# A prefix log-sum-exp whose stores move from SyncE's DMA ring to ScalarE's

## The chip, the cores and the metric

The kernel runs on one core of a Trainium2 chip. The core has a matrix engine (TensorE, PE in the profile), a vector engine (VectorE, DVE), an engine for activation functions (ScalarE, ACT), GpSimd (POOL) and SyncE (SP), which here only starts transfers. Transfers between the large memory (HBM) and the on-chip memory are carried by 16 DMA engines. The metric is the time on the device in microseconds (us), as the median of several executions; lower is better.

## The reference

```python
# x: (4, 4096, 4128) float32
out[:, 0, :] = x[:, 0, :]
for t in range(1, S):
    mx = np.maximum(out[:, t - 1, :], x[:, t, :])
    out[:, t, :] = mx + np.log(np.exp(out[:, t - 1, :] - mx) + np.exp(x[:, t, :] - mx))
```

For each of 4 batches and each of 4128 columns, the output at position t is the logarithm of the sum of the exponentials of all inputs up to t. Input and output are 270.5 MB each.

## The kernel before

A batch has 4096 rows. They are cut into **steps** of 384 rows (128 partitions with R = 3 consecutive rows each) and one of 256 rows per batch (2 rows per partition): 11 steps per batch, 44 in all. In the first batch the short step comes first, in the others last, so steps 0, 21, 32 and 43 are short. A step is one tile `xt` of 128 partitions x 3 x 4128 float32 in the pool `xpool`, which has 4 buffers. The load fills the tile, the exponentials are written over it as 16-bit numbers (the view `half`), the logarithms are written over it again as float32, and the store reads it: one buffer serves a step from the start of its load to the end of its store.

The columns of a step are cut into 4 **chunks** of 1024, the last with a tail of 32 columns more. For a chunk,

- `exp` (L128) is one ScalarE instruction over the chunk's columns of all rows of the step;
- `head` (L132 to L142) sums over the partitions on TensorE into a PSUM tile `pt`, with triangular matrices of ones, and adds the carry of the step before through the matrix `pick`;
- `stage(j)` (L159 to L170) takes the logarithm of row j on ScalarE (L162), then adds the next row's exponentials to `pt` with an identity matrix. The last stage lets VectorE save the running sum in `carry` as two 16-bit parts (`keep`, L92 and L93). In the last chunk, stage 0 also takes the logarithms of the tail (L167).

The order is written out by hand (`manual_schedule`, L85): each engine executes its instructions in the order in which the program emits them. The loop at L192 goes over the chunks of all steps in one sequence. In turn g it emits stage 2 of chunk g-2, stage 1 of chunk g-1 and stage 0 of chunk g, then the exp of chunk g+2, then the head of chunk g+1. So when the last stage of a step's last chunk is emitted, ScalarE's queue already holds before it the exps of the first three chunks of the next step.

Behind the last stage of a step's last chunk stand the step's store and the load of a later step. Before the change both are issued by SyncE, through one DMA ring. Three loads are issued at the start; then load k+3 follows store k on SyncE (L198 to L200). SyncE also works in order: store k waits there until ScalarE has written the last logarithms of step k, and load k+3 stands behind it. Load k+3 uses the buffer of step k-1, so it also waits until store k-1 has landed.

The lines that matter: `load` L109 to L113, `store` L115 and L116, `exp` L126 to L130, `stage` L159 to L170, the first loads L185 to L187, the loop L192 to L205. Transfers are named here by step: load k fills, store k empties the tile of step k.

Of the kernel before, what the change touches and what calls it, by code (L numbers as in the profile page):

```python
# [49 lines left out]
def kernel(  # L50
# [11 lines left out]
    nc = tc.nc  # L62
# [11 lines left out]
    bufs = 4  # L74
# [23 lines left out]
    class Step:  # L98
# [14 lines left out]
            nc.sync.dma_start(out=self.xt, in_=self.dram(x))  # L113

        def store(self):  # L115
            nc.sync.dma_start(out=self.dram(out), in_=self.xt)  # L116

    class Chunk:
        def __init__(self, step, c):
# [52 lines left out]
    steps = []  # L172
# [9 lines left out]
        assert row == S  # L182

    chunks = [Chunk(s, c) for s in steps for c in range(n_main)]
    ahead = bufs - 1  # L185
    for s in steps[:ahead]:
        s.load()  # L187
    stored = 0
    chunks[0].exp()
# [2 lines left out]
    for g in range(len(chunks) + R - 1):  # L192
        for d in range(R - 1, -1, -1):
            if 0 <= g - d < len(chunks) and d < chunks[g - d].t.r:
                k = chunks[g - d]
                k.stage(d)
                if k.c == last and d + 1 == k.t.r:
                    k.t.store()  # L198
                    if stored + ahead < len(steps):
                        steps[stored + ahead].load()  # L200
                    stored += 1
        if g + 2 < len(chunks):
            chunks[g + 2].exp()
        if g + 1 < len(chunks):
            chunks[g + 1].head()  # L205
# [30 lines left out]
```

The softmax here doesn't subtract the row's maximum and nothing guards it: scores larger than these inputs give would overflow.

## Time and profile before

| what | value |
|---|---|
| median of 4 runs | 1263.11 us (1262.47 to 1263.28) |
| profiled execution: its time, its span | 1263.0 us, 1261.3 us |
| busy: ScalarE, TensorE, VectorE | 947.1 us (75%), 688.2 us (55%), 451.5 us (36%) |
| moved | 270.53 MB read, 270.53 MB written, 429 GB/s over the span |
| load of a full step, issue to landing | 42.2 us (median of 40), 6192 KB |
| store of a full step, issue to landing | 28.1 us (median of 40), 6192 KB |
| exp of a chunk of a full step (L128) | 2.77 us; waits for loads 247.7 us in all |
| logarithm of one row of a chunk (L162) | 1.03 us, 512 of them |

The span runs from the first to the last instruction that the profile shows; the execution's own time is 1.7 us longer. An engine's idle time is put down to what ended it. "SPq" is SyncE's queue: its instructions only start transfers, and its waits are shown apart. A line of the timeline has the start, the duration, engine, source line, operation and tiles; in square brackets stands the idle time before it and what ended it. A line of the chain of waits gives shares of the span along the one chain of work that ended last. A line of stretches has the window, its length, the busy time of PE, PE's weight load, DVE, ACT and POOL with their numbers of instructions, the granted TensorE clock, the busy share of the DMA engines and the rate in GB/s.

### The profile page before, as it was taken

The numbers are of one execution on the slowest core, as the hardware profiler recorded it, in microseconds if no ns is written. First come the engines' busy times: TensorE is split into PE (matmuls) and PEld (weight loads), VectorE is DVE, ScalarE is ACT, GpSimd is POOL, SyncE is SP. The second block draws the span as 40 slices with busy tenths as digits, with TensorE's granted clock in tenths as the row PEclk, the third lists the DMA queues.
The fourth block names the chain that finished last, engine by engine and source line by source line (L and its number), as shares of the span: only waits on it lengthen the run. The fifth ranks groups of instructions, "written<-read, shape, count | busy, mean of one in ns | idle before, by whom it ended". The sixth has DMA issues, their size and how long they took to land.

```text
span 1261.3 us, 6165 instructions
## 1 busy us (share of the span) xinstructions
PE 688.2 (55%) x2268; PEld 236.1 (19%) x2268; DVE 451.5 (36%) x445; ACT 947.1 (75%) x733; POOL 2.2 (0%) x13
## 2 busy tenths in 40 slices
PE   3665554565455555555356555555634655555562
PEld 1222111121112111111112121111211211121120
DVE  2443333333333333334424333333442433333344
ACT  5997777777777777778569777777966977777784
POOL 0000000000000000000000000000000000000000
PEclk9887777777787787787768777778767877777776
DMA  9999999999999999999999999999999999999998
GB/s 411 409 431 440 431 428 432 437 431 430 436 434 433 430 437 433 429 431 433 436 431 440 430 429 435 434 431 435 431 432 435 430 430 435 437 430 431 433 423 347
DMA packets 12702, 541.46 MB, mean 429 GB/s; under 512 B 1408, under 2 KB 1408, under 8 KB 1408
## 3 DMA queue, kind: packets, MB, share of 16 engines
q1 hardware_dynamic: 12672, 541.07, 99.4%
q8 instruction: 18, 0.29, 0.1%
q14 instruction: 12, 0.10, 0.0%
HBM read 270.53 MB, written 270.53 MB: 429 GB/s over the span
## 4 chain that ended last, share of the span: by engine, by line
DMA 70%; ACT 21%; PE 5%; issue 2%; DVE 1%; SPq 0%; ACTq 0%
DMA xt<-in_x_dram 67%; ACT xt L128 11%; ACT xt L162 10%; PE pt L88 5%; DMA out_dram<-xt 2%; DVE carry L92 0%; DVE carry L93 0%; ACT xt L167 0%; SPq L116 0%; ACTq L231 0%; SPq L113 0%; ACTq L128 0%; PE qt L88 0%
## 5 line engine op out<-in xcount | busy, mean ns | idle before, releaser
L128 ACT ACTIVATE xt<-xt 128x3072 f16<-128x3072 f32 (+3 forms) x176 | 478.5, 2719 | 247.7 <-DMA xt<-in_x_dram 247.7
L88 PE MATMUL pt<-xt,ident 128*128 128x512 f16 x672 | 249.9, 468 | 531.0 <-ACT xt L162 530.4
L162 ACT ACTIVATE xt<-pt 128x1024 f32<-128x1024 f32 x512 | 487.5, 1030 | 3.0 <-PE pt L88 1.2
L92 DVE CAST carry<-pt 32x1024 f16<-32x1024 f32 x176 | 216.5, 1230 | 761.3 <-ACT xt L162 761.1
L88 PE MATMUL pt<-xt,excl 128*128 128x512 f16 x672 | 247.3, 504 | 0.0
L93 DVE TENSOR_TENSOR carry<-pt,carry 32x1024 f16<-32x1024 f32 x176 | 215.9, 1227 | 6.1
L88 PEld LDWEIGHTS <-ident 128*128 128x128 f16 x672 | 69.9, 104 | 677.3 <-issue 652.9
L88 PE MATMUL pt<-xt,incl 128*128 128x512 f16 x352 | 152.0, 526 | 23.9 <-ACT xt L128 15.1
L88 PEld LDWEIGHTS <-excl 128*128 128x128 f16 x756 | 92.1, 124 | 140.6 <-issue 107.2
L88 PE MATMUL pt<-carry,pick 128*128 128x512 f16 x320 | 110.2, 430 | 0.0
L88 PEld LDWEIGHTS <-incl 128*128 128x128 f16 x480 | 44.7, 111 | 131.2 <-DVE carry L93 95.4
L88 PEld LDWEIGHTS <-pick 128*128 128x128 f16 x360 | 40.7, 113 | 57.5 <-issue 35.3
L167 ACT ACTIVATE xt<-qt 128x96 f32<-128x96 f32 (+1 forms) x44 | 10.9, 248 | 45.8 <-PE pt L88 45.8
L92 DVE CAST carry_t<-qt 32x32 f16<-32x32 f32 x44 | 8.7, 197 | 25.4 <-ACT xt L167 25.2
L88 PE MATMUL qt<-xt,incl 128*128 128x64 f16 (+2 forms) x128 | 12.4, 196 | 0.0
L88 PE MATMUL qt<-xt,excl 128*128 128x64 f16 (+1 forms) x84 | 10.6, 187 | 0.0
L93 DVE TENSOR_TENSOR carry_t<-qt,carry_t 32x32 f16<-32x32 f32 x44 | 8.5, 193 | 1.5
L88 PE MATMUL qt<-carry_t,pick 128*128 128x96 f16 (+1 forms) x40 | 8.2, 205 | 0.0
L83 DVE MEMSET carry<- 128x512 uint32 x4 | 1.9, 485 | 1.1 <-PEq L220 1.0
L70 ACT ACT_TABLE_LOAD x1 | 1.3, 1283 | 0.8 <-PEq L220 0.8
L35 POOL TENSOR_SCALAR_AFFINE_SELECT pick<-pick 128x128 f16<-128x128 f16 x2 | 0.6, 292 | 0.1
L25 POOL TENSOR_SCALAR_AFFINE_SELECT incl<-incl 128x128 f16<-128x128 f16 x1 | 0.3, 292 | 0.0
(11 smaller groups left out, 1.9 us busy)
## 6 DMA issues: line engine op xcount, KB each, us to landing
xt<-in_x_dram SPq DMA_DIRECT2D x40, 6192.0 KB, 42.2
out_dram<-xt SPq DMA_DIRECT2D x40, 6192.0 KB, 28.1
xt<-in_x_dram SPq DMA_DIRECT2D x4, 4128.0 KB, 37.1
out_dram<-xt SPq DMA_DIRECT2D x4, 4128.0 KB, 23.0
```

The source lines that it names most:

```text
L25: nc.gpsimd.affine_select(out=t, in_=t, pattern=[[1, P]], compare_op=mybir.AluOpType.is_ge, fill=0.0, base=base, channel_multiplier=-1,)
L35: nc.gpsimd.affine_select(out=t, in_=t, pattern=[[step, P]], compare_op=mybir.AluOpType.not_equal, fill=1.0, base=base, channel_multiplier=1,)
L70: nc.scalar.preload_act_table_set("natural_log_exp_and_others")
L83: nc.vector.memset(t, 0.0)
L88: nc.tensor.matmul(pt, lhsT=w, rhs=rhs, start=start, stop=stop, skip_group_check=True)
L92: nc.vector.tensor_copy(cr[HI:HI + 32, :], pt[HI:HI + 32])
L93: nc.vector.tensor_tensor(out=cr[LO:LO + 32, :], in0=pt[HI:HI + 32], in1=cr[HI:HI + 32, :], op=mybir.AluOpType.subtract,)
L128: nc.scalar.activation(self.t.half[:, :, 2 * c0:2 * c0 + w], self.t.xt[:, :, c0:c0 + w], ACT.Exp,)
L162: nc.scalar.activation(t.xt[:, j, c * CH:(c + 1) * CH], pt, ACT.Ln)
L167: nc.scalar.activation(t.xt[:, :, t0:D], self.qt, ACT.Ln)
```

## The change

Stores are issued by ScalarE, in its own instruction queue and through its own hardware DMA ring; loads stay with SyncE. All four buffers are loaded at the start, and the load that follows store k is load k+4, into the very buffer that store k empties. SyncE's queue then holds nothing but loads, and each waits only for the store of its slot to land. A store stands on ScalarE behind the last logarithm of its step and ahead of the rest of that turn's work.

```diff
         def store(self):
-            nc.sync.dma_start(out=self.dram(out), in_=self.xt)
+            nc.scalar.dma_start(out=self.dram(out), in_=self.xt)
 ...
     chunks = [Chunk(s, c) for s in steps for c in range(n_main)]
-    ahead = bufs - 1
-    for s in steps[:ahead]:
+    for s in steps[:bufs]:
         s.load()
 ...
                     k.t.store()
-                    if stored + ahead < len(steps):
-                        steps[stored + ahead].load()
+                    if stored + bufs < len(steps):
+                        steps[stored + bufs].load()
                     stored += 1
```

## The prediction

> **What bounds the kernel now.** I read the page first, for the DMA engines' share and rate, then the chain of waits, then SyncE's own waits, then the timelines of SyncE and ScalarE around one step, and last the stretches at the end.
>
> ```profile
> span 1261.3 us, 6165 instructions
> DMA  9999999999999999999999999999999999999998
> q1 hardware_dynamic: 12672, 541.07, 99.4%
> DMA 70%; ACT 21%; PE 5%; issue 2%; DVE 1%; SPq 0%; ACTq 0%
> ```
>
> All 16 DMA engines are busy in every slice, and the one ring that carries loads and stores fills 99.4% of them. The packet records of the same trace (no view prints them one by one) say how full that is: of 10,240 packets of 49,536 bytes the median takes 1.829 us and the next starts 1.826 us after, so 16 engines move 16 x 49,536 / 1.826 = 434 GB/s at best. Each engine carries 8 packets of each transfer: 80 transfers of 3 rows per partition at 8 x 1.826 = 14.61 us and 8 of 2 rows at 8 x 1.219 = 9.75 us make 1168.6 + 78.0 = 1246.6 us. The first packet starts at 1.8 us, the last ends at 1260.0. So the slowest engine has 1260.0 - 1.8 - 1246.6 = 11.6 us beyond its packets, and none of the idle time shown below: instruction fetches (30 packets on queues 8 and 14, each holding its engine up by 0.6 to 1.5 us) and slow packets. The other 15 lose less there and instead stand idle for 0.1 to 7.0 us (4.3 us in the mean) at about 1230, as the stretches show (last columns: PE clock, DMA share, GB/s):
>
> ```profile
> 1225.00:1230.00 5.00, 2.46 (x10) 0.79 (x9) 2.38 (x5) 4.32 (x5) 0.00 (x0) 1.00 0.80 347
> 1230.00:1235.00 5.00, 4.06 (x10) 1.27 (x10) 2.92 (x3) 5.00 (x6) 0.00 (x0) 0.66 0.50 211
> 1235.00:1240.00 5.00, 2.51 (x11) 0.90 (x11) 4.87 (x5) 4.47 (x4) 0.00 (x0) 1.00 0.76 327
> ```
>
> Then the waits on SyncE, and one step on SyncE and ScalarE:
>
> ```profile
> SPq L116 <- ACT xt L162: 1179.2, 44, 30.0
> SPq L113 <- DMA out_dram<-xt: 14.4, 4, 4.9
> ```
> ```profile
> 204.18 0.34 SPq L116 DMA_DIRECT2D out_dram<-xt  x1
> 204.62 0.39 SPq L113 DMA_DIRECT2D xt<-in_x_dram  x1
> 233.64 0.34 SPq L116 DMA_DIRECT2D out_dram<-xt  x1
> ```
> ```profile
> 217.81 2.76 ACT L128 ACTIVATE xt<-xt 128x3072 f16<-128x3072 f32 x1 [6.21 <-DMA xt<-in_x_dram]
> 247.50 2.76 ACT L128 ACTIVATE xt<-xt 128x3072 f16<-128x3072 f32 x1 [6.44 <-DMA xt<-in_x_dram]
> ```
>
> SyncE stands at a store for nearly the whole span, and the next load stands behind it. That looks like the loss, but it isn't one: a store goes out every 29.3 us and lands 28.1 us after its issue (the issue table's median), so the slot of the next load comes free 29.3 - 28.1 = 1.2 us before the store that it stands behind. ScalarE waits 6.4 us per step for a load, because 2 x 14.61 = 29.2 us of transfer per step is more than its own 23 us.
>
> One thing in the order matters later: store k comes late. Load 8 lands at 217.81 and store 7 is issued at 233.64, 15.8 us after it, because ScalarE's order has three exps of step k+1 ahead of the last Ln of step k.
>
> **What the Trainium skill says.** "DMA: Bandwidth & Descriptors", section "Where 436 GB/s comes from": 435 GB/s is the ceiling of the 16 engines; the trace's 434 agrees. Section "Issuing engines are not separate DMA queues": transfers from ScalarE and SyncE run on the same 16 engines and interleave, and a second issuer saves only issue time, here 44 x 0.34 us on SyncE, which is idle. Section "Queues, rings and completion order": an engine goes round the rings that have work, packet by packet. In this trace only instruction fetches show it. "Perfetto Trace Analysis", section "DMA Optimizations", advises separate issuers for input and output for flexibility; this trace shows little for that to free.
>
> **The change part by part.**
>
> *Four loads at the start instead of three.* The engines are busy from 1.8 us either way, and store 0 can't go before 37.2 us, when load 2 is still running. Load 3 moves ahead of store 0; bytes are only reordered. Nothing. Without the cover of full engines it would be worth the 0.4 us of one issue.
>
> *Loads no longer stand behind stores on SyncE.* Worth at most those 1.2 us of lead per load, hidden by the transfers already queued.
>
> *Load k+4 waits for store k to land.* Worked out with the two rings sharing each engine equally: when store k lands, load k+4 is issued and store k+1 is the other stream. Each needs 14.6 us of engine, so both take about 29 us. The load ring runs dry for some 2 us per step (landing 0.6, issue 0.3, first packet 0.85, the last as at the end of this trace: store 42 issued 1233.88, first packet 1234.72), in which the store has the engines alone. The engines run dry only if store k+1 isn't there when store k ends. It is issued 15.8 us after load k+2 lands, and that load ends some 27 us before store k does: 11 us in hand. So the period stays 29.2 us. Nothing.
>
> *44 store issues on ScalarE.* 0.34 us each and about 0.15 us (estimate) for its own last Ln to be written: 44 x 0.5 = 22 us of ScalarE. Behind each stand the Ln and exp of the next chunks, and TensorE and VectorE behind these. The 6.4 us of waiting per step take it. Nothing; with no such idle time it would be 22 us. No store can block ScalarE for its slot's sake, since it waits only for ScalarE's own results; SyncE issued three loads in a row in 1.32 us without being held.
>
> *The end.* Time 0 is store 39's last packet. Load 43 (2 rows, 9.8 us) starts at 1.8; store 40 has 12.8 left by then. Sharing, load 43 ends at 21.4 and lands at 22.0; store 40 ends at 24.4, store 41 (14.6) at 39.0. Store 42 is issued 12.9 us after load 43 lands (1220.94 to 1233.88 before): 22.0 + 12.9 + 0.85 = 35.8, so 3.2 us early. Then 53.7 and, with store 43, 63.4: no gap. If load 42 still has 5 us ahead of load 43, load 43 lands at 30.0, store 41 ends at 43.9 and store 42 starts at 43.8: just in time. The gap at 1230 closes for the 15 engines that have it, but the slowest never had it, and the end is its end. Nothing.
>
> *Reads and writes mixed.* Now an engine alternates load and store packets. Inside the old ring the turn from load to store costs only the 6 ns of the end marker. In about half of the old packets (49%) some engines were already loading while others stored, since the engines drift 4 to 7 us apart: after 60 us these packets exceed the median by 6.0 ns, the others by 2.1. All packets mixed instead of half: 704 packets per engine x 3.9 x 0.51 = +1.4 us. Bounds: 0 if the difference is only that of the fetches among them, and for the alternation itself the rival below.
>
> Sum: profiled execution 1263.0 (span 1261.3 and 1.7 around it; the runs' median is 1263.1), + 0 + 0 + 0 + 0 + 0 + 1.4, on the median: 1264.5.
>
> **The rivals.**
>
> *Alternating rings costs time (slower).* Place: every packet boundary on every engine. The trace has a foreign ring cutting in 29 times: after each instruction fetch the next data packet takes 2.08 to 2.49 us instead of 1.83. Were that 0.25 us the price of every return, 704 x 0.25 = 176 us and 1439 us would result. Against: going into a fetch costs nothing (8192 bytes in 309 ns, the full rate), so I put the delay down to the fetch's own target. It decides from 2.5 / 704 = 3.6 ns per packet. I let the range hold a tenth of the 250, 25 ns: 17.6 us, 1280.7.
>
> *Stores win the sharing (slower).* If stores went first, load 43 would wait for store 40 and for store 41 from its issue at 16, land at about 38, and store 42 would start at 52 instead of 39: +13 us, 1276. For it: the margin of the last step is 0 to 3 us. Against: the equal turns that the skill describes.
>
> *The slowest engine gets rid of its excess (faster).* If fetches and slow packets fell evenly on the engines, the end would come 4.3 us sooner, at 1258.8; all 11.6 us are the limit, 1251.5. For it: other interleaving may shift who is delayed. Against: the instructions and so the fetches stay the same. Full-duplex use of an engine would give far more, but no overlap shows at any of the 40-odd turns from load to store.
>
> **How the numbers follow.** Likeliest case, engines full at the old packet price: 0.55, 1261 to 1267 around 1264.5. Costly alternation 0.23, stores ahead 0.10, less excess 0.12. Faster or slower by 0.2% (2.5 us) is about what a measurement tells from no change; 0.10 of the likeliest case's 0.55 lies beyond 1265.6. So faster 0.12, same 0.45, slower 0.43. The range runs from 1258.5 (the evened-out excess) to 1281 (25 ns per packet); 5 in 100 below, 10 above.
>
> **What would show it.** Right: two rings of about half the engines' time each, DMA at 9 in all slices, ScalarE still waiting 5 to 6 us per step at L128 for loads, loads landing about 29 us after issue, stores up to 40. Packets above 1.83 us net of sharing mean costly alternation; a gap around the last three stores means stores ahead; an 8 in the middle slices means that the coupling of load k+4 to store k starves the rings. Wrong altogether if ScalarE shows long waits at its store issues.

## The result

The changed kernel takes 1265.36 us in the median of 33 runs against 1262.93 us for 54 runs of the kernel before, measured side by side. The ratio of the mean times, without the one run at 1286.29 us that counts as slow, is 1.003, 95% interval 1.0021 to 1.0039; the medians differ by 0.2%. So the change is a small loss, and the forecast of 1264.5 us is 0.9 us off. The runs do something that the forecast does not speak of. Before, all 54 lie between 1262.47 and 1263.41 us. After, the lowest is 1263.60 us, ten of 33 lie above 1268 us, and the highest is at 1286.29 us. So there are two things to explain: a floor 0.8 us higher (profiled execution 1263.83 us against 1263.0), and a spread above that floor, which did not exist before and makes most of the difference in the median.

### The profile page after: what moved, and what is told of

The parts are those of the page before. It is cut to its first block, busy times and chain, and to the rows that moved or that the text cites. A ratio compares the mean times of both kernels' runs of the same rounds, so it can differ in the third digit from the quotient of the medians.

```text
span 1262.1 us, 6084 instructions
## 1 busy us (share of the span) xinstructions
PE 684.9 (54%) x2268; PEld 241.3 (19%) x2268; DVE 451.5 (36%) x445; ACT 951.9 (75%) x733; POOL 2.2 (0%) x13
## 4 chain that ended last, share of the span: by engine, by line
DMA 75%; ACT 20%; PE 3%; issue 0%; DVE 0%; ACTq 0%; SPq 0%
DMA xt<-in_x_dram 40%; DMA out_dram<-xt 35%; ACT xt L128 11%; ACT xt L162 9%; PE pt L88 3%; ACT xt L167 0%; ACTq L116 0%; DVE carry L92 0%; DVE carry L93 0%; SPq L113 0%; ACTq L128 0%; PE qt L88 0%
## 5 line engine op out<-in xcount | busy, mean ns | idle before, releaser
L128 ACT ACTIVATE xt<-xt 128x3072 f16<-128x3072 f32 (+3 forms) x176 | 476.6, 2708 | 226.4 <-DMA xt<-in_x_dram 226.4
L88 PE MATMUL pt<-xt,ident 128*128 128x512 f16 x672 | 254.0, 476 | 540.7 <-ACT xt L162 540.3
L162 ACT ACTIVATE xt<-pt 128x1024 f32<-128x1024 f32 x512 | 492.4, 1024 | 22.0 <-ACT xt L162 12.9
L92 DVE CAST carry<-pt 32x1024 f16<-32x1024 f32 x176 | 216.5, 1230 | 763.3 <-ACT xt L162 763.2
L88 PEld LDWEIGHTS <-incl 128*128 128x128 f16 x480 | 49.3, 113 | 118.6 <-DVE carry L93 72.1
```

Of the source, the lines that this page charges most:

```text
L88: nc.tensor.matmul(pt, lhsT=w, rhs=rhs, start=start, stop=stop, skip_group_check=True)
L92: nc.vector.tensor_copy(cr[HI:HI + 32, :], pt[HI:HI + 32])
L128: nc.scalar.activation(self.t.half[:, :, 2 * c0:2 * c0 + w], self.t.xt[:, :, c0:c0 + w], ACT.Exp,)
L162: nc.scalar.activation(t.xt[:, j, c * CH:(c + 1) * CH], pt, ACT.Ln)
```

## The profile after

The page of the changed kernel: the span, the DMA share and rate in 40 slices, the two rings, the chain, and the two waits on ScalarE that the change touches.

```profile
span 1262.1 us, 6084 instructions
DMA  9999999999999999999999999999999999999997
q1 hardware_dynamic: 6336, 270.54, 49.8%
q10 hardware_dynamic: 6336, 270.54, 49.6%
DMA 75%; ACT 20%; PE 3%; issue 0%; DVE 0%; ACTq 0%; SPq 0%
L128 ACT ACTIVATE xt<-xt 128x3072 f16<-128x3072 f32 (+3 forms) x176 | 476.6, 2708 | 226.4 <-DMA xt<-in_x_dram 226.4
L162 ACT ACTIVATE xt<-pt 128x1024 f32<-128x1024 f32 x512 | 492.4, 1024 | 22.0 <-ACT xt L162 12.9
```

Queue 1 now carries the loads and queue 10, ScalarE's ring, the stores. Each fills half of the engines' time, together 99.4% as the one ring did. The DMA engines stand at 9 in all slices but the last. ScalarE's idle time before L162 grew from 3.0 to 22.0 us: that is the 44 store issues with the wait for the last logarithm before each. Its waiting for loads fell by about the same amount, from 247.7 to 226.4 us. Here is one store of it:

```profile
1213.45 1.04 ACT L162 ACTIVATE xt<-pt 128x1024 f32<-128x1024 f32 x1
1214.52 0.34 ACTq L116 DMA_DIRECT2D out_dram<-xt  x1
1214.91 1.94 ACT L162 ACTIVATE xt<-pt 128x1024 f32<-128x1024 f32 x2 [0.42 <-ACT xt L162]
```

The packet records answer the question of what it costs an engine to alternate. A packet is what one engine moves in one piece, here the rows of one partition: 49,536 bytes in a full step. Around 300 us load and store packets pass through each engine mixed; on 15 of the 16 engines every one of them takes 1.829 us, on the other one up to 1.861. What a packet takes beyond its median is called its excess below. Over the whole run the excess is 5.0 us per engine against 4.7 before.

SyncE waits at the loads now. From issue to landing a store takes longer than before (36.0 us, it was 28.1) and a load less (35.0 us, it was 42.2):

```profile
SPq L113 <- DMA out_dram<-xt: 1165.8, 40, 53.8
```
```profile
xt<-in_x_dram SPq DMA_DIRECT2D x40, 6192.0 KB, 35.0
out_dram<-xt ACTq DMA_DIRECT2D x40, 6192.0 KB, 36.0
```

Last, the stretches around 1230 us, where the engines were idle before:

```profile
1225.00:1230.00 5.00, 2.96 (x17) 1.09 (x16) 2.85 (x4) 4.32 (x6) 0.00 (x0) 1.00 0.92 396
1230.00:1235.00 5.00, 2.65 (x10) 0.89 (x10) 2.46 (x2) 5.00 (x5) 0.00 (x0) 1.00 0.07 23
1235.00:1240.00 5.00, 2.14 (x6) 0.80 (x6) 4.42 (x4) 4.55 (x5) 0.00 (x0) 0.82 0.74 317
```

The gap did not close. It moved and deepened: from 1230 to 1235 nearly nothing moves (23 GB/s). Before, the 16 engines were idle here for 0 to 7.0 us, 4.1 in the mean; now it is 1.2 to 6.4 us, 5.3 in the mean. No engine is spared any more, and that is the higher floor. Before, the engine with the most excess had 10.2 us of it and no idle time; now the one with the most has 10.6 us and 1.2 us of idle time. Store 42 is issued at 1235.48 instead of 1233.88, and the last packet ends at 1260.9 instead of 1260.0.

The timeline of ScalarE says why store 42 is late. These are three first exps of a step (L128) and the stores 41 and 42 between them:

```profile
1198.68 2.76 ACT L128 ACTIVATE xt<-xt 128x3072 f16<-128x3072 f32 x1 [5.41 <-DMA xt<-in_x_dram]
...
1214.52 0.34 ACTq L116 DMA_DIRECT2D out_dram<-xt  x1
...
1222.62 1.91 ACT L128 ACTIVATE xt<-xt 128x2048 f16<-128x2048 f32 x1 [0.15 <-DMA xt<-in_x_dram]
...
1235.48 0.34 ACTq L116 DMA_DIRECT2D out_dram<-xt  x1
```

and the same two exps before the change:

```profile
1196.42 2.76 ACT L128 ACTIVATE xt<-xt 128x3072 f16<-128x3072 f32 x1 [6.16 <-DMA xt<-in_x_dram]
...
1221.02 1.91 ACT L128 ACTIVATE xt<-xt 128x2048 f16<-128x2048 f32 x1 [1.35 <-DMA xt<-in_x_dram]
```

After the change ScalarE waits only 0.15 us for load 43. From the landing of load 42 on it works nearly without a pause: 15.8 us to store 41 and 21.0 us more to store 42. So the end hangs on load **42**, which lands 2.3 us later than before (1198.68 against 1196.42). Of this, 1.2 us come back, since ScalarE no longer waits 1.35 us for load 43, and the wait at store 41 adds 0.4 us: 2.3 - 1.2 + 0.4 = 1.5, of the 1.6 us seen. What delays load 42 was not followed further.

## The experiments

Every run had a kernel before beside it on the same chip, with a median of 1262.87 to 1262.94 us.

**The changed kernel four more times.** No edit. The theories are the end (T), starvation in the middle (M) and, from the third on, disturbance between loads and stores (H).

> The changed kernel as it is, to see its spread. Theory T (the end): every run has its 16 engines full until about 1230 and the loss lies between the landing of load 43 and the issue of store 42; runs differ by when load 43 lands, so the median is 1264 to 1266, a run in four lies above 1269, and in any profile the end is load 43's landing plus 38.4 to 39 us. Rival M (starvation in the middle): long runs show idle DMA engines in the middle slices, at a load that waits for the store of its slot, and the end is as in the short runs.

> The changed kernel once more, for a second trace of it. As for the rerun before: by theory T the end is load 43's landing plus 38.4 to 39 us whatever the time, by rival M idle engines in the middle slices.

> The changed kernel once more, for a trace of a long run: if it lies above 1266 us, rival M wants idle engines in the middle slices, theory H packets longer than 1.829 us and no idle ones. At 1263.7 it tells nothing new.

> The changed kernel once more for a trace of a long run: above 1266 us, theory H wants packets longer than 1.829 us in a stretch of the middle, rival M idle engines there. Near 1264 it tells nothing new.

rerun_a had a median of 1266.12 us in 8 runs (1263.92 to 1269.55), with the ratio 1.0028 (1.0018 to 1.0038): spread and shift are there again, though theory T wanted one run in four above 1269 us and one in eight is. Its profiled run took 1263.92 us; rerun_b, rerun_c and rerun_d took 1263.73, 1264.53 and 1264.07. None of the traces is of a long run. What they do show is where their small differences come from. In none of them do the engines stand idle in the middle; the end is alike (store 42's issue to the end differs by under 0.2 us); what differs is the time of slow packets. It follows one class of packets, which the packet records yield when the order of packets on each engine is rebuilt from their starts and ends: those whose position in their transfer (0 to 7 on an engine, counted round, so that 0 is one above 7) is the same as, or one above, that of the other ring's packet just before.

| run | time, us | excess of these packets, us per engine |
|---|---|---|
| rerun_b | 1263.73 | 0.21 |
| after | 1263.83 | 0.18 |
| rerun_a | 1263.92 | 0.62 |
| rerun_d | 1264.07 | 0.77 |
| rerun_c | 1264.53 | 1.30 |

Of rerun_c's 1.30 us, 0.59 fall between 900 and 1000 us, where rerun_b has 0.01. The same records say which packets these are. All but one of those in rerun_c are the first packet of a store, right behind the last packet of a load, and 1.28 of its 1.30 us lie in five stores, 1, 19, 30, 33 and 41. Their first packets come 1.8 to 3.3 us after the store's issue, where the median is 4.6 us. So they are starts of transfers, and not packets that run side by side with those of the other ring. That a store begun soon after its issue has a long first packet is a reading of these traces that no run tested.

So M has no support here. H has some only in this: packets that are long, and no idle engines. These five runs say nothing on the long ones.

**Store 40 behind load 43.** If sharing the engines with store 40 is what holds load 43 up, letting load 43 go first should free the end.

```diff
-        def store(self):
-            nc.scalar.dma_start(out=self.dram(out), in_=self.xt)
+        def store(self, ring):
+            ring.dma_start(out=self.dram(out), in_=self.xt)
 ...
-                    k.t.store()
+                    k.t.store(nc.sync if stored == len(steps) - bufs else nc.scalar)
```

> One store, that of step 40, is issued by SyncE behind load 43 instead of by ScalarE; all else as in the changed kernel. Theory T: loads 42 and 43 then run alone for about 9 us, load 43 lands some 8 to 10 us sooner after its issue, store 42 is there before store 41 ends, the idle stretch before the last two stores is gone and the slowest engine's own work sets the end: 1260.3 to 1262.5 us, runs within 1.5 us of each other. Rival M: the spread stays, median 1264 to 1266 with runs above 1269.

Median 1265.77 us, 21 runs from 1265.14 to 1285.61, ratio 1.0038 (1.0022 to 1.0053). Load 43 landed at 1207.9 instead of 1222.5 us, 14.6 us sooner where 8 to 10 were expected, and the gap before the last stores is gone. But the time rose, the lowest run by 1.5 us, so theory T as I had put it is wrong: first, because a new gap opened where store 40 used to be, and second, because store 42 hardly moved (1233.23):

```profile
1190.00:1195.00 5.00, 2.70 (x7) 0.85 (x7) 2.46 (x2) 2.87 (x4) 0.00 (x0) 0.74 0.18 79
1195.00:1200.00 5.00, 1.88 (x12) 0.84 (x11) 0.01 (x1) 3.72 (x3) 0.00 (x0) 0.84 1.06 409
...
1230.00:1235.00 5.00, 3.60 (x9) 1.07 (x8) 2.92 (x3) 4.58 (x5) 0.00 (x0) 0.66 1.06 459
```
```profile
1212.12 0.34 ACTq L116 DMA_DIRECT2D out_dram<-xt  x1
...
1233.23 0.34 ACTq L116 DMA_DIRECT2D out_dram<-xt  x1
```

From store 41 to store 42 it is 21.1 us again although load 43 landed more than 10 us before ScalarE needed it: that stretch is ScalarE's own work. And the spread stayed, with six of 21 runs above 1268 us, so the spread does not come from the end.

**One row of store 40 kept in front.** The store is cut: the first row of each partition on ScalarE, to fill the new gap, the other two behind load 43.

```diff
-            nc.scalar.dma_start(out=self.dram(out), in_=self.xt)
+            o, h = self.dram(out), 1 if split else self.r
+            nc.scalar.dma_start(out=o[:, :h], in_=self.xt[:, :h])
+            if split:
+                nc.sync.dma_start(out=o[:, h:], in_=self.xt[:, h:])
 ...
-                    k.t.store()
+                    k.t.store(stored == len(steps) - bufs)
```

> As the changed kernel, but of store 40 only the first row of each partition is issued by ScalarE (4.9 us of transfer), the other two rows by SyncE behind load 43. The row keeps the engines at work while SyncE waits for store 39. If the end limits the floor: no idle stretch at 1195 and none at 1236, the slowest engine's work sets the end, lowest run 1261.0 to 1262.8 us. If it doesn't: lowest run 1263.6 us or more, as in the changed kernel. The median lies 1 to 3 us above the lowest in either case, as that comes from elsewhere.

Median 1264.35 us, lowest 1263.13, highest 1282.75, ratio 1.0021 (1.0006 to 1.0035). The lowest run falls between the two expectations. The gap at 1195 is closed:

```profile
1195.00:1200.00 5.00, 1.48 (x12) 0.74 (x11) 0.00 (x0) 2.51 (x1) 0.00 (x0) 0.93 1.05 433
...
1230.00:1235.00 5.00, 2.65 (x10) 0.89 (x10) 2.91 (x3) 4.58 (x5) 0.00 (x0) 1.00 0.71 301
```

At 1235 the engines are idle for 2.2 us in the mean instead of 5.3, and the engine with the most excess (10.6 us, as in the changed kernel) not at all instead of 1.2. The lowest run is 0.5 us below that of the changed kernel (1263.13 against 1263.60), but the two profiled runs differ by less than 0.1 us (1263.77 and 1263.83), since in row_behind the excess of all engines is larger, 6.9 us in the mean. So this fits an end that sets the floor and leaves about half a microsecond to be had there; it doesn't prove it. The kernel is still not faster than the one before.

**The wait alone, on one ring.** Load k+4 behind store k as in the change, but all on SyncE.

```diff
         def store(self):
-            nc.scalar.dma_start(out=self.dram(out), in_=self.xt)
+            nc.sync.dma_start(out=self.dram(out), in_=self.xt)
```

> The wait of the change alone: load k+4 behind store k, but both on SyncE's ring. If the second ring is only another way to the same engines and the new pacing is harmless by itself: within 0.5% of before, 1258 to 1269 us. My theory: store k is then the last thing in the ring when load k+4 waits for its landing, so the ring runs dry for landing 0.6, issue 0.3 and first packet 0.85, 1.75 us on each of 40 steps, and the engines' spread of a few us is added to each: 1263 + 70 to 1263 + 200, so 1330 to 1460 us; the second ring is what covers the wait.

1434.67 us, ratio 1.1361 (1.1346 to 1.1375), inside what my theory gave. Load and store are now issued in one go when a store has landed, and the ring behind is empty:

```profile
305.68 0.33 SPq L113 DMA_DIRECT2D xt<-in_x_dram  x1
306.10 0.38 SPq L116 DMA_DIRECT2D out_dram<-xt  x1
338.53 0.33 SPq L113 DMA_DIRECT2D xt<-in_x_dram  x1
338.95 0.38 SPq L116 DMA_DIRECT2D out_dram<-xt  x1
```

The period is 32.9 us instead of 29.2. The packet records split the loss: 105.8 us idle per engine, 2.6 us on each of 40 steps (1.75 was the estimate without the engines' spread), and 76 us of slow packets (4.7 before), of which I had none in the sum. The new wait is thus expensive when loads and stores share one ring and one queue, and moving the stores is what hides it. Which of the two counts, the ring or the queue, was not separated: in SyncE's order store k+1 stands behind load k+4 and is held up with it. The waits on SyncE show that most stores were ready by then, since only 9 of 44 still waited for their logarithms there:

```profile
SPq L113 <- DMA out_dram<-xt: 1293.9, 40, 34.1
SPq L116 <- ACT xt L162: 61.4, 9, 25.2
```

The two halves of the change are not independent: the later loads cost 13.6% where stores and loads share one queue and ring, and next to nothing once the stores have moved.

**The transfers without the computation.** Is the disturbance a matter of the two rings? The loop was replaced by transfers alone; stores read a fixed tile. free_one_ring differs from free_rings only in that SyncE issues the stores too.

```diff
+    for s, l in zip(steps, steps[bufs:] + steps[:bufs]):
+        nc.scalar.dma_start(out=s.dram(out), in_=fixed[:, :s.r, :])
+        l.load()
```

> Transfers alone, without the computation: 44 loads on SyncE into three rotating buffers and 44 stores of a fixed tile on ScalarE, no transfer waits for one of the other ring. The sum of the packets is 1246.6 us, with the slowest engine's fetches and the ends about 1255 to 1260. Rival M (the spread comes from the wait of a load for the store of its slot): runs within 1 us of each other. Theory H (reads and writes in two rings disturb each other in memory by chance): runs spread by 5 to 20 us as in the changed kernel.

> The same transfers without the computation, loads and stores in turn in SyncE's one ring. Both theories: runs within 1 us of each other, 1253 to 1260 us. It is the base for the two free rings; two rings should be within 3 us of it at their floor if turning from ring to ring costs nothing.

Two rings: 1462.27 us (1458.88 to 1463.91), against 1272.11 us (1271.56 to 1273.06) for one. That is 15% for the second ring, far more than either expectation had; the runs spread by 5 us, so this pair doesn't tell M from H. The one ring is 12 us above its expectation as well: its first transfer is issued at 13.9 us, since the stored tile has to be filled first (10.4 us), which I had left out.

```profile
DMA  9999999999999999999999999999999999999996
GB/s 401 381 374 377 374 371 382 370 375 374 373 377 373 374 371 370 355 377 362 378 405 370 373 369 369 368 361 374 373 380 396 370 370 370 369 370 352 353 346 274
q10 hardware_dynamic: 6336, 270.54, 50.3%
q1 hardware_dynamic: 6336, 270.54, 48.0%
```

The engines are busy throughout and move 370 GB/s instead of 426. It is the packets: the loads take 2.06 us in the mean and the stores 2.18, where the same packets in the changed kernel take 1.84 and 1.83. So two rings can cost a great deal, and the changed kernel escapes that almost wholly. Why?

**Paced, far apart, and two rings of loads.** Three edits to the free rings: a store waits for the store before it (VectorE rewrites one element of the fixed tile in between), with two load buffers; loads 20 steps ahead instead of 3 (the expectation speaks of 4, the code of free_rings has 3); loads on both rings.

```diff
         nc.scalar.dma_start(out=s.dram(out), in_=fixed[:, :s.r, :])
+        nc.vector.memset(fixed[:, 0, 0:1], 0.0)        # paced_rings
 ...
-    for s, l in zip(steps, steps[bufs:] + steps[:bufs]):
+    for s, l in zip(steps, steps[20:] + steps[:20]):   # free_far
 ...
-        nc.scalar.dma_start(out=s.dram(out), in_=fixed[:, :s.r, :])
+        nc.scalar.dma_start(out=other[:, :s.r, :], in_=s.dram(x))   # two_load_rings
```

> The two rings without the computation, but paced: a store waits for the landing of the store before it, and at most two loads are out, so that the engines meet again at every step. Two free rings took 1462 us with packets of 2.06 to 2.18 us. If drifting apart is what makes the packets long: packets back at 1.83 us, 1265 to 1285 us (10 us are the filling of the stored tile). If alternating loads and stores on an engine without the computation's pace is slow in itself: 1430 us or more.

> The two free rings with loads 20 steps ahead of the stores instead of 4. If the places in memory that are read and written at the same time matter (4 steps apart against 20): below 1400 us. If not: 1440 to 1480 us, as with 4.

> Both rings carry loads: SyncE and ScalarE each load all of the input into buffers of their own, two out at a time on each ring, and only a sixteenth-partition piece is stored at the end. The same number of packets. If going from ring to ring costs: 1400 us or more. If only loads beside stores disturb each other: 1250 to 1265 us, packets 1.83 us.

free_far took 1455.97 us (1454.37 to 1457.58): the distance in memory by steps hardly matters. two_load_rings took 1263.52 us (1263.21 to 1263.87): going from ring to ring costs nothing while both carry loads. paced_rings took 1386.93 us, between its two expectations, and its slices show that it is two things in one run:

```profile
DMA  9999999999999888899999989899999989989998
GB/s 398 435 434 435 432 430 434 430 422 417 421 430 403 332 326 328 332 402 434 418 404 429 384 344 355 325 341 410 431 402 410 432 347 374 344 321 344 390 390 374
```

It runs at 398 to 435 GB/s for about 450 us, falls to 330 for about 140 us, comes back to 434, falls again; in all it has 75 us of slow packets and 58 us of idle time per engine. In the slow stretches the end markers of a load and of a store come at the same microsecond (528 and 528, 567 and 567 us), in the quick ones mostly not (67 and 75, 91 and 108). That led me to sort store packets by how many positions they are ahead of the load packet just before them on the same engine. Each cell has the mean excess over 1.829 us, and the number of packets. Positions are counted round here too, so the column 1 of the changed kernel's two rows holds the first packets of stores from above. The cells of free_rings and free_far with few packets depend on how the order is rebuilt, and nothing rests on them.

| positions ahead | 0 | 1 | 2 | 3 | 4 |
|---|---|---|---|---|---|
| paced_rings | 261 ns (1677) | 33 ns (58) | 0 ns (296) | 10 ns (291) | 1 ns (306) |
| free_rings | 356 ns (4319) | 363 ns (136) | 59 ns (106) | (4) | (3) |
| free_far | 323 ns (4483) | 370 ns (102) | 186 ns (10) | | |
| after | (1) | 19 ns (149) | 2 ns (1263) | 1 ns (2209) | 0 ns (418) |
| rerun_c | | 104 ns (200) | 2 ns (1453) | 1 ns (1994) | 0 ns (424) |
| two_load_rings, second ring | 1 ns (5120) | | | | |

A packet is one partition's rows, so the same position in two transfers of one shape is the same partition of the tiles, if the engine goes through both in the same order. When an engine loads and stores at the same position in turn, its store packets take 14 to 20% longer, and the load packets of the two free runs take 2.06 and 2.09 us in the mean, 13 to 14% longer. From two positions apart on, the excess is 0 to 10 ns in paced_rings and 0 to 2 ns in the changed kernel. Two loads at the same position cost nothing. The free rings start together and stay together. In the changed kernel stores run mostly two to three positions ahead, out of reach. This comes from sorting what the runs happened to do; no run set the distance on purpose, and why the changed kernel has the distance that it has was not followed up.

## Why the prediction was right, and where not

**The sum.** That 1264.5 lies so near 1265.36 us is luck in its parts. The mixing of reads and writes was put at 1.4 us, and 0.3 was measured; the end was put at nothing and took 0.9; the spread, which is 1.5 us between the profiled run and the median, was in no term. What is right, and not by luck, is that the other parts cost nothing because the DMA engines are full before and after.

**What bounds the kernel.** Right: the engines' own packets. Nothing that the change freed on SyncE came out as time. Two readings need setting right. The 11.6 us of the slowest engine were counted from the first packet of any engine; its own starts at 2.5 us, and what it has beyond its packets is 10.2 us of slow packets and 0.3 us of an instruction fetch, so on this engine the fetches hardly count. And the 435 GB/s of the Trainium skill ("DMA: Bandwidth & Descriptors", section "Where 436 GB/s comes from") are those of the 16 ports into the on-chip memory; for transfers between HBM and on-chip memory the same section has the HBM side bind, at about 358. The 429 GB/s over the span here are above that, so the measurement decides. No run here shows which part of the path sets the 1.829 us of a packet.

**Four loads at the start; loads no longer behind stores.** Costed at nothing, and nothing is seen of them. The first slices move 410 and 411 GB/s against 411 and 409 before.

**The wait of load k+4.** Costed at nothing with two rings, and 11 us in hand. The cost is right; the way there is not quite. The load ring was to run dry for some 2 us per step, and loads were to land 29 us after their issue. They take 35.0, because the ring doesn't run dry: load 7 is issued at 154.8 us and load 6 has packets until 160.3, and from load 4 on every load is issued at least 2.6 us before the last packet of the load before it. The stores have less in hand than was thought: store 5 is issued at 176.6 us and store 4 lands at 183.9, so 7.3 us, and the least before the last three stores is about 2 us (store 19). one_ring_late shows what happens when a store is held up with the load.

**Store issues on ScalarE.** The estimate was 0.5 us each, 22 us in all, hidden. The idle time before L162 grew by 19.0 us, and the waiting for loads fell by 21.3.

**The end.** Here the step failed in a small way. It kept one clock for 16 engines: store 40 with 12.8 us left when load 43 starts. In the store ring the engines are 8.6 to 10.3 us apart by stores 38 to 40 (7.4 in the one ring before), so the early engines had finished store 41 by 1230 and stood. Counted from store 39's last packet, the forecast's second case has store 41 end at 43.9 us and store 42 start at 43.8; store 42 started at 42.5, even a little sooner, but store 41 ended at 36.2 to 41.3, depending on the engine. The forecast also tied store 42 to load 43's landing, while ScalarE's own 21 us after store 41 decide. Costed at nothing, it took 0.9 us.

**Reads and writes mixed.** Costed at 1.4 us. The packets' excess grew by 0.3 us per engine in the profiled run and by 1.3 in rerun_c, and there it is the first packets of five stores. So the term is wrong where it was measured, and where the size fits, it fits by accident. In the runs without the computation, what counts is not whether loads and stores are mixed among the engines but whether they stand at the same position on one engine.

**Alternating rings costs time.** This rival was given 0.23. It is wrong for the profiled runs (0 to 1.3 us), and its evidence, the slow packet after an instruction fetch, was no measure of it: two rings of loads alternate 5120 times at 1 ns. But the rival's price exists, 0.26 to 0.36 us per store packet, under a condition that I hadn't thought of. The range reached up to a tenth of 0.25 us per packet, and runs up to 1278.67 us lie in it.

**The spread.** No step of the forecast had it. It isn't the end (last_behind and row_behind keep it), and it isn't TensorE's clock, which was granted at 0.77 to 0.79 in short and long runs alike. The small differences between the five traced runs follow the long first packets of a few stores. A long run could be one in which the rings fall into step for a few transfers, as they do for 140 us at a time in paced_rings; a step of 29.2 us at 330 instead of 434 GB/s would add 9 us. That is an argument: no long run was traced, and the short ones show no such stretch. Nor was it tried whether the stores on ScalarE bring the spread without the later loads. Its cause stays open.

**Stores ahead; less excess.** Load 43 landed at 1222.5 and not near 1232, and the most excess on one engine went from 10.2 to 10.6 us; neither rival came.

## What to carry to other kernels

Where the DMA engines are full with large packets, a second ring for the stores freed nothing here: ask first how long the slot of the next load has been free when the load is issued (here 1.2 us). Splitting a stream over two rings also replaces a fixed order by one that comes out of timing, and here the fixed order had the even run times, 0.9 us from the lowest to the highest against 22.7 us with two rings. When loads and stores of the same shape do share the engines from two rings, look at the packets' duration, and not only at the engines' busy share, which is 9 in nearly all slices of free_rings too. If the packets are long, running loads and stores at different positions is the thing to try; no run here tried it on purpose.

## What was not expected of the hardware

- Load and store packets of 49,536 bytes that alternate on an engine at the same position in their transfers take 2.06 and 2.18 us in the mean instead of 1.83 (370 against 426 GB/s). Whether the place is the partition of the on-chip memory or the rows in HBM was not separated: the position is the same in both. The steps' distance in HBM makes little difference (20 steps: 1456 us, 3 steps: 1462).
- This can come and go within a run: 434, then 330 GB/s for 140 us, then 434.
- In one_ring_late, where the engines meet at each step, it is the first and the last packet of each load that are long, by 0.75 and 1.03 us in the mean, and at no position do the store packets exceed their median by more than 4 ns in the mean. This was not followed up.
